# A hybrid layer's input projection: token rows at another stride, one more block scaled late, weight splits ahead of finishing, and finishing in two steps

## The chip, the cores and the metric

The kernel runs on one core of one Trainium2 chip. The metric is the device time of one execution in microseconds, given as the median of several runs; a profiled execution, taken apart from those runs, gives the trace. Five engines work from queues of their own, in order: PE (TensorE, matrix products; its weight loads are listed as PEld), DVE (VectorE), ACT (ScalarE), POOL (GpSimd) and SP (SyncE, which here only issues transfers). Transfers run on 16 DMA engines; loads are issued by SP, stores by POOL.

## The reference

One inference step of one decoder layer for 4096 new tokens and 64 sample tokens (8 sequences of 8), model width 1024, all in fp32:

```
h = rmsnorm(x) * g_pre
z = h @ w_in                      # (4160, 1024) @ (1024, 2816)
out_a = silu(cg) * cb * conv3(cc * ch)            # 256 channels
out_b = silu(ag) * window_attention(q, k, v)      # window 128, 8 heads of 64, 2 kv heads, a sink each
out_c = silu(mg) * memory_attention(mq)           # 4 heads of 64, 256 memory tokens
y = [out_a, out_b, out_c] @ w_out                 # (4160, 1024) @ (1024, 1024)
x = x + rmsnorm(y) * g_post
```

Results are the new x, the keys and values of the last window, the convolution's state, and the memory's keys and values. The result has to be near fp32, so every product of the kernel is made from a number's high part (rounded to the fp32r type) and the rest, three products for one: high by high, high by low, low by high.

## The kernel before

**Two halves.** The first, up to about 1066 us, is the input projection; the second is attention and output projection, ordered by the framework's scheduler. In the first half the order on all engines is written out by hand (a list of numbered steps, each with loads and jobs), and this is where most of the change lies.

**The projection.** The tokens (64 sample tokens first) are five blocks of 832, each two halves of 416. The 22 column tiles of 128 are taken in six groups of up to four (line `GROUPS`): gates (tiles 14 to 17), two convolution groups (0 to 7), memory and attention queries (18 to 21), a one-pair group with keys and values (12, 13), and gates and queries (8 to 11). For each block and group, a step p = 0 to 6 is one of the seven products of Strassen's scheme (in Winograd's form): a sum of weight blocks (A11, S2, A12, S3, S1, A22, S4) by a sum of token blocks (B11, T2, B21, T3, T1, T4, B22). A step has 12 products for each of two column pairs q, on the line that the profile calls L603, 128x416 outputs each; the one-pair group has 12. The first group of the first block is made in eight plain steps instead.

**Weights.** In block 0, and in the first group of block 1, the four raw weight blocks are loaded, POOL and DVE make the sums (`sums`, L166 to L168; `last_sum`, L173), ACT casts to the high part and DVE subtracts (`split_w`, L140 and L141), and POOL stores the split sums (`fill_sum`). Later blocks load the split sums (`load_split`, L153) and split only A11, A12 and A22 (`fill`). Weight buffers go round in a ring of six, two per step.

**Tokens.** During block b-1, the rows of block b are loaded and squared (ACT, L245), POOL makes 1/rms of each (`row_factors`) and stores it (tensor `rowd`), SP loads it back broadcast to all partitions (`row_spread`, L255), and DVE multiplies the transposed tokens by gain and factor (`x_scale`, L199). Then come the sums T1 to T4 and the splits (L218, L219) into `x1`, places of 4 rows of 416 high parts followed by 4 rows of 416 low parts. Block 0 is *unscaled*: ACT applies the gain only (`x_gain`), and DVE multiplies the results by the factors (`z_rows`, L260).

**Ends of steps and groups.** At the end of a step, the accumulators go into z tiles of a ring of three, two for each group: ACT copies at p = 0 and 2 (L612, L616), DVE adds at the others (L610). Finishing a group's z tile is, for gates, tanh (ACT) and a product (DVE), for queries and keys a rounded copy (ACT, L279) and the difference (DVE, L281); POOL stores both. The tile `which=1` is finished at step p = 6 of its group, `which=0` in the step after. For block 0 the sample tokens' columns are also copied to a small buffer `zs`. Within a step, SP gets the step's loads; then come the q = 0 products, half of the jobs (finishing first, then splits and token work), the q = 1 products, the rest of the jobs, and the eviction. So a job that waits holds up everything behind it on its engine, evictions too.

**Block 4** carries the memory's projection and the first chunk of the attention as pieces between its steps (`plan_third`), and near its end the output weights are loaded and split.

The jobs of a step, in `step`, and how the sums of a group that begins at step `s0` are placed, in `plan_weights`:

```
jobs = [*first.pop(i, ()), *jobs_at.pop(i, ())]
half = (len(jobs) + 1) // 2
...
job_at(s0 - 2, *(lambda k=k: split_keep(k) for k in key("A11")))
job_at(s0 - 1, *(lambda b=b, g=g, q=q: sums(b, g, q) for q in qs))
job_at(s0 - 1, *(lambda k=k: fill_sum(k) for k in key("S2")))
```

## Time and profile before

| | |
|---|---|
| median of 3 runs | 1687.2 us (1682.62 to 1687.97) |
| profiled execution | 1681.09 us, span 1679.3 us |
| mean granted clock of PE | 0.967 |
| PE busy | 1552.4 us, 8489 products |
| DVE, ACT, POOL busy | 1012.0, 729.4, 428.8 us |
| input projection | to 1066.5 us |

How rows are read: a row of a group gives line, engine, operation, output and inputs, shape and count, then busy time and mean ns of one, then the idle time just before and what ended it. A row of the timeline is start, length, the same names, and in brackets the idle time before it and what released it. A row of a table by stretch gives the stretch, its length, busy time and count of PE, PEld, DVE, ACT and POOL, the granted clock of PE, the DMA engines' mean busy share, and GB/s.

### The profile page before, as it was taken

The numbers are of one execution on the slowest core, as the hardware profiler recorded it, in microseconds if no ns is written. First come the engines' busy times: TensorE is split into PE (matmuls) and PEld (weight loads), VectorE is DVE, ScalarE is ACT, GpSimd is POOL, SyncE is SP. The second block draws the span as 40 slices with busy tenths as digits, with TensorE's granted clock in tenths as the row PEclk, the third lists the DMA queues.
The fourth block names the chain that finished last, engine by engine and source line by source line (L and its number), as shares of the span: only waits on it lengthen the run. The fifth ranks groups of instructions, "written<-read, shape, count | busy, mean of one in ns | idle before, by whom it ended". The sixth has DMA issues, their size and how long they took to land.

```text
span 1679.3 us, 23937 instructions
## 1 busy us (share of the span) xinstructions
PE 1552.4 (92%) x8489; PEld 1403.4 (84%) x8489; DVE 1012.0 (60%) x1743; ACT 729.4 (43%) x1864; POOL 428.8 (26%) x667
## 2 busy tenths in 40 slices
PE   8799587997999989998998988799999999999998
PEld 8698477997999889997997987678888888888876
DVE  3877587445744466445745544576666666666653
ACT  7434234242433233232432333466565656556542
POOL 1345223001100101001002022363444444444310
PEclk9899798999999999998999999899999999999999
DMA  9468855699677986799787668998767867876332
GB/s 250 162 229 237 279 196 200 220 272 314 230 270 240 276 301 236 233 303 268 252 291 182 197 222 233 288 168 162 159 146 151 166 136 155 167 159 148 126 126 88
DMA packets 167516, 354.30 MB, mean 211 GB/s; under 512 B 21253, under 2 KB 90149, under 8 KB 167365
## 3 DMA queue, kind: packets, MB, share of 16 engines
q1 hardware_dynamic: 116069, 242.06, 48.1%
q0 software_dynamic: 50896, 110.19, 26.8%
q8 instruction: 67, 1.10, 0.3%
q10 hardware_dynamic: 432, 0.53, 0.1%
q14 instruction: 52, 0.43, 0.1%
HBM read 262.93 MB, written 90.77 MB: 211 GB/s over the span
## 4 chain that ended last, share of the span: by engine, by line
PE 44%; issue 2%; DMA 2%; DVE 1%; ACT 1%; POOL 0%; SPq 0%; DVEq 0%; POOLq 0%; ACTq 0%
PE y L1235 21%; PE c L603 8%; PE ws L1003 3%; PE wo L845 2%; PE wt L1026 2%; PE xs L939 2%; PE xt L954 2%; PE wo L975 2%; PE wo L981 1%; DMA vT<-vd 1%; PE mem_acc L517 1%; DMA gpost<-in_gpost 0%; DMA kst<-qd 0%; DMA qd<-zh 0%; DVE z L610 0%
## 5 line engine op out<-in xcount | busy, mean ns | idle before, releaser
L603 PE MATMUL c<-x,w_0S 128*128 128x416 f32 x1392 | 303.9, 370 | 73.3 <-DMA w_0S<-wd_0S 28.6
L1235 PE MATMUL y<-x 128*128 128x512 f32 (+1 forms) x1296 | 369.0, 399 | 0.0
L603 PEld LDWEIGHTS c<-x,w_0S 128*128 128x128 f32 x1392 | 274.4, 200 | 87.2 <-ACT w_0S L140 34.7
L1235 PEld LDWEIGHTS y<-x 128*128 128x128 f32 x1296 | 238.2, 189 | 46.1 <-issue 1.6
L603 PE MATMUL c<-x,w_0A 128*128 128x416 f32 x1140 | 241.4, 362 | 26.7 <-ACT z L612 18.9
L603 PEld LDWEIGHTS c<-x,w_0A 128*128 128x128 f32 x1140 | 219.6, 195 | 35.1 <-ACT z L612 21.4
L610 DVE TENSOR_TENSOR z<-c,z 128x832 f32<-128x832 f32 (+1 forms) x145 | 137.2, 946 | 164.7 <-PE c L603 158.9
L603 PE MATMUL c<-x,w_1S 128*128 128x416 f32 x1152 | 236.4, 354 | 0.0
L603 PEld LDWEIGHTS c<-x,w_1S 128*128 128x128 f32 x1152 | 218.8, 191 | 2.8 <-issue 0.4
L603 PE MATMUL c<-x,w_1A 128*128 128x416 f32 x960 | 196.4, 354 | 0.0
L603 PEld LDWEIGHTS c<-x,w_1A 128*128 128x128 f32 x960 | 180.9, 190 | 2.8 <-issue 1.2
L141 DVE TENSOR_TENSOR w_0A<-wr_0A,w_0A 128x512 fp32r<-128x512 f32 x91 | 64.8, 712 | 121.1 <-ACT w_0A L140 121.1
L1016 ACT ACTIVATE sm<-sm,wnm 128x128 f32<-128x128 f32 x256 | 99.5, 390 | 63.5 <-DVE wnm L1010 63.4
L948 POOL TENSOR_SCALAR xp<-xp,xrd 128x256 f32<-128x256 f32 x128 | 75.9, 601 | 179.2 <-DVE xrd L944 179.1
L1235 PE MATMUL y<-x,parts 128*128 128x512 f32 (+1 forms) x264 | 101.6, 385 | 0.0
L140 ACT CAST w_0A<-wr_0A 128x512 fp32r<-128x512 f32 x91 | 55.9, 616 | 78.9 <-PE c L603 39.1
L940 DVE TENSOR_REDUCE xmx<-xs 128x2 f32<-128x512 f32 x64 | 44.0, 687 | 59.3 <-PE xs L939 59.3
L127 POOL DMA_DIRECT2D md<-th x30 | 16.3, 543 | 246.3 <-DVE th L298 215.9
L1028 ACT COPY wpt<-wt 128x512 f32<-128x512 f32 x64 | 37.1, 583 | 96.0 <-PE wt L1026 95.9
L245 ACT ACTIVATE nat<-nat 104x1024 f32<-104x1024 f32 x40 | 42.3, 1057 | 80.9 <-DMA nat<-in_x_p 78.8
L1003 PEld LDWEIGHTS ws<-kst,q 128*128 128x128 f32 x512 | 70.9, 193 | 7.3 <-DVE z L610 1.5
L1003 PE MATMUL ws<-kst,q 128*128 128x256 f32 x512 | 73.4, 286 | 1.1 <-DVE z L610 1.1
(258 smaller groups left out, 2317.2 us busy)
## 6 DMA issues: line engine op xcount, KB each, us to landing
w_0S<-wd_0S SPq DMA_DIRECT2D x92, 512.0 KB
w_1S<-wd_1S SPq DMA_DIRECT2D x76, 512.0 KB
wr_0A<-in_w_in SPq DMA_DIRECT2D x102, 256.0 KB
q<-qd POOLq DMA_DIRECT2D x64, 384.0 KB, 7.9
wr_1A<-in_w_in SPq DMA_DIRECT2D x85, 256.0 KB
mix<-md SPq DMA_DIRECT2D x16, 1024.0 KB
xr<-in_x_p SPq DMA_DIRECT2D x32, 512.0 KB
nat<-in_x_p SPq DMA_DIRECT2D x39, 416.0 KB
```

Source lines behind the costliest of these rows:

```text
L140: S.copy(w[:, 0], raw)
L141: V.tensor_tensor(w[:, 1], raw, f(w[:, 0]), op=ALU.subtract)
L245: S.activation(t[:RG], t[:RG], AF.Square, accum_out=factors[b][:RG, i : i + 1])
L603: TE.matmul(bank[:, :HW], l, r, start=first and i == 0, stop=last and i == 3 * KH - 1, skip_group_check=more)
L610: add = lambda dst, other: V.tensor_tensor(dst, c, other, op=ALU.add)
L845: TE.matmul(o[cs], v[:, cs], p, start=i == 0, stop=i == n - 1, tile_position=(0, 64 * half))
L940: V.tensor_reduce(mx[:, :nb], s, axis=AX.X, op=ALU.max)
L948: G.tensor_scalar(p[:, i, :], p[:, i, :], rd[:, i : i + 1], 0.5, op0=ALU.mult, op1=ALU.mult)
L1003: TE.matmul(s3[:, hh, :], self.q[:, 4 + 2 * (2 * half + hh) + kvh, i * P : i * P + P], self.kst[:, 2 * kvh + part, i * P : i * P + 2 * P], ...
L1016: S.activation(sm[:, hh, :], sm[:, hh, :], AF.Exp, bias=nm[:, hh : hh + 1], scale=SCALE, accum_out=den[:, hh : hh + 1])
L1028: S.copy(pt, t)
L1235: TE.matmul(acc, self.hl[l][:, k], wo[k][c0 // 512][:, r, c0 % 512 : c0 % 512 + c1 - c0], start=j == 0, stop=j == passes * KT - 1)
```

## The change

1. The split tokens lie in places of their own for high and low parts, each of 4 rows of 448 floats (1792 bytes) of which 416 are used. All moving and all stationary operands of L603 then start at the same address modulo 256.
2. Block 1 is unscaled as well: gains on ACT, `z_rows` on DVE when its groups are finished; its factors are loaded back in its own first group. For blocks 2 to 4 the factors are made at step p = 6 of the second convolution group and loaded back three steps later; the rows are loaded three steps earlier, and the token loads are cut in two and spread over eight steps.
3. Weight splits form a list of their own, first in each step. The sums are made one step earlier, beside A11's split.
4. Finishing takes two steps: rounding or tanh at p = 6 (tile 1) and p = 0 of the next group (tile 0), difference or gate a step later each. The convolution takes four steps.
5. The small copies for sample tokens go; nine loads and two additions late in the attention (`sample_tokens`) take their place.
6. In block 4, the first attention chunk is loaded one step earlier and its pieces begin one step later and follow closer; the second chunk is loaded three steps earlier; output weights' loads and splits are spread otherwise.

```diff
-XS = 2 * KH * HW
+
+XR = 448
+XS = KH * XR
+UNSCALED = 2
...
     def slot(i):
-        return (x6[:, :] if i == 6 else x1[:, i * XS : (i + 1) * XS]).rearrange("p (a k n) -> p a k n", a=2, k=KH)
+        places = [x1[:, n * XS : (n + 1) * XS] for n in range(11)] + [x6[:, n * XS : (n + 1) * XS] for n in range(3)]
+        return [t.rearrange("p (k n) -> p k n", k=KH)[:, :, :HW] for t in places[2 * i : 2 * i + 2]]
...
-    def finish_parts(b, z, idx, zsi):
+    def finish_parts(b, z, idx):
...
-        hi = temp(f"zh{b}_{idx}")[:, :BW].bitcast(F32R)
-        S.copy(hi, z)
-        lo = z.bitcast(F32R)
-        V.tensor_tensor(lo, z, f(hi), op=ALU.subtract)
-        store(f(qd[0, idx, :, tokens(b)]), f(hi))
-        store(f(qd[1, idx, :, tokens(b)]), f(lo))
+        made = []
+
+        def round_():
+            if idx == 0 and b == NBLK - 1:
+                kl = temp("kl")
+                S.copy(kl[:, :P], z[:, BW - P :])
+                store(a["o_kp"], kl[:, :P])
+            hi = temp(f"zh{b}_{idx}")[:, :BW].bitcast(F32R)
+            made.append(hi)
+            S.copy(hi, z)
+            store(f(qd[0, idx, :, tokens(b)]), f(hi))
+
+        def rest():
+            lo = z.bitcast(F32R)
+            V.tensor_tensor(lo, z, f(made[0]), op=ALU.subtract)
+            store(f(qd[1, idx, :, tokens(b)]), f(lo))
+        return round_, rest
+
+    def finish_gate(b, z, idx):
         z = flat(z)
-        th = temp(f"th{b}_{idx}")[:, :BW]
-        S.activation(th, z, AF.Tanh, scale=0.5)
-        V.scalar_tensor_tensor(th, th, 1.0, z, op0=ALU.add, op1=ALU.mult)
-        if b == 0:
-            V.tensor_copy(zs[:, zsi, :], th[:, :NS])
-        store(md[idx, :, tokens(b)], th)
+        made = []
+
+        def tanh():
+            th = temp(f"th{b}_{idx}")[:, :BW]
+            made.append(th)
+            S.activation(th, z, AF.Tanh, scale=0.5)
+
+        def gate():
+            th = made[0]
+            V.scalar_tensor_tensor(th, th, 1.0, z, op0=ALU.add, op1=ALU.mult)
+            store(md[idx, :, tokens(b)], th)
+        return tanh, gate
...
-                    job_at(s0 - 2, *(lambda k=k: split_keep(k) for k in key("A11")))
-                    job_at(s0 - 1, *(lambda b=b, g=g, q=q: sums(b, g, q) for q in qs))
-                    job_at(s0 - 1, *(lambda k=k: fill_sum(k) for k in key("S2")))
-                    job_at(s0, *(lambda k=k: split_keep(k) for k in key("A12")), *(lambda b=b, g=g, q=q: last_sum(b, g, q) for q in qs))
+                    fill_at(s0 - 2, *(lambda k=k: split_keep(k) for k in key("A11")), *(lambda b=b, g=g, q=q: sums(b, g, q) for q in qs))
+                    fill_at(s0 - 1, *(lambda k=k: fill_sum(k) for k in key("S2")))
+                    fill_at(s0, *(lambda k=k: split_keep(k) for k in key("A12")), *(lambda b=b, g=g, q=q: last_sum(b, g, q) for q in qs))
...
-                t = s(2, 0) + i
+                t = s(2, 0) - (3 if b > 1 else 0) + i
                 load_at(t, lambda i=i, b=b: row_load(RJ * b + i))
                 job_at(t + 1, lambda i=i, b=b: row_square(RJ * b + i))
-            job_at(s(3, 2), lambda b=b: row_factors(b))
-            load_at(s(3, 4), lambda b=b: row_spread(b))
+            factors_at, spread_at = (s(2, 6), s(3, 2)) if b >= UNSCALED else (s(3, 2), at[b, 0, 4])
+            job_at(factors_at, lambda b=b: row_factors(b))
+            load_at(spread_at, lambda b=b: row_spread(b))
             for i, o in enumerate(("B11", "B12", "B22", "B21")):
-                load_at(s(3, 1 + i), lambda b=b, o=o: x_load(b, o))
-            for t, o in ((s(3, 6), "B11"), (s(4, 1), "B12"), (s(4, 3), "B22"), (s(4, 5), "B21")):
-                job_at(t, lambda b=b, o=o: x_scale(b, o))
+                for k in range(2):
+                    load_at(s(2, 6) + 2 * i + k + (2 if b == 1 else 0), lambda b=b, o=o, k=k: x_load(b, o, 2 * k, 2 * k + 2))
+            for t, o in ((s(3, 4), "B11"), (s(3, 6), "B12"), (s(4, 2), "B22"), (s(4, 5), "B21")):
+                job_at(t, lambda b=b, o=o: (x_scale if b >= UNSCALED else x_gain)(b, o))
...
-        load_at(n0 + 12, first_chunk)
+        load_at(n0 + 11, first_chunk)
         for n in range(21):
-            third_at(13 + n, lambda: third["chunk"].pop(0)())
-        load_at(n0 + 34, lambda: chunk_load(1))
+            third_at(14 + n * 4 // 5, lambda: third["chunk"].pop(0)())
+        load_at(n0 + 31, lambda: chunk_load(1))
         end = at[NBLK - 1, NG - 1, 0]
-        for p, js in enumerate(((), (0, 1), (2, 3), (4, 5), (6, 7, 8), (9, 10, 11, 12), (13,), (14, 15))):
+        for p, js in ((-1, (0, 1)), (0, (2, 3)), (3, (4, 5, 6, 7)), (4, (8, 9, 10, 11)), (6, (12, 13, 14, 15))):
             for j in js:
-                load_at(end + p - 2, lambda j=j: wo_load(j))
+                load_at(end + p, lambda j=j: wo_load(j))
+        for p, js in enumerate(((), (0, 1), (2, 3), (), (4, 5), (6, 7, 8), (9, 10, 11), (12, 13, 14, 15))):
+            for j in js:
                 job_at(end + p, lambda j=j: wo_split(j))
...
-                n = at[0, 1, 0] if (b, g) == (0, 0) else at[b, g, NP_ - 1] + 1
...
-                scale = lambda which: [lambda b=b, z=z: z_rows(b, z(which))] if b == 0 else []
-                done = lambda which, b=b, g=g, z=z: [lambda: [fn() for fn in finish(b, g, which, z(which))]]
+                scale = lambda which: [lambda b=b, z=z: z_rows(b, z(which))] if b < UNSCALED else []
...
-                    if b == 0:
-                        front_at(n - 1, *scale(1))
-                    front_at(n, *scale(0), make, run(0))
-                    front_at(n + 1, run(1), run(2))
-                elif (b, g) == (0, 0):
-                    front_at(n, *scale(1), *done(1))
-                    front_at(n + 1, *scale(0), *done(0))
+                    front_at(n, *scale(1))
+                    front_at(n + 1, *scale(0), make)
+                    back_at(n + 1, run(0))
+                    front_at(n + 2, run(1))
+                    front_at(n + 3, run(2))
                 else:
-                    front_at(n - 1, *scale(1), *done(1))
-                    front_at(n, *scale(0), *done(0))
+                    for k, which in enumerate((1, 0)):
+                        made = []
+                        make = lambda made=made, b=b, g=g, which=which, z=z: made.extend(finish(b, g, which, z(which)))
+                        run = lambda j, made=made: lambda: [fn() for fn in made[j]]
+                        front_at(n + k, *scale(which), make)
+                        back_at(n + k, run(0))
+                        front_at(n + k + 1, run(1))
...
-        jobs = [*first.pop(i, ()), *jobs_at.pop(i, ())]
+        jobs = [*fills_at.pop(i, ()), *first.pop(i, ()), *back.pop(i, ()), *jobs_at.pop(i, ())]
...
+    def sample_tokens():
+
+        lo = work([P, 4, P], "sm", "zs_lo").rearrange("p a n -> p (a n)")[:, : 7 * NS].rearrange("p (a n) -> p a n", n=NS)
+        cols = lambda x: x[:, :, :NS].rearrange("j p n -> p j n")
...
+        V.tensor_tensor(zs[:, 0:5], zs[:, 0:5], lo[:, 0:5], op=ALU.add)
+        V.tensor_tensor(zs[:, 10:12], zs[:, 10:12], lo[:, 5:7], op=ALU.add)
```

How the order moves, at three places. First POOL where block 1's first group begins (`wr_0` are its raw weights, `w_5` and `z_5` belong to block 0's last group, `wd` are stored sums, `md` and `qd` the results). Before:

```order
L127 DMA md<-th_3_1914 128x832
L127 DMA qd<-zh_2_1920 128x832
L127 DMA qd<-z_5_1_1700 128x832
L166 TENSOR_TENSOR wr_0_0A_1821<-wr_0_0A_1785,wr_0_0A_1821 128x512
L167 TENSOR_TENSOR wr_0_0A_1785<-wr_0_0A_1744,wr_0_0A_1785 128x512
L166 TENSOR_TENSOR wr_0_1A_1823<-wr_0_1A_1787,wr_0_1A_1823 128x512
L167 TENSOR_TENSOR wr_0_1A_1787<-wr_0_1A_1746,wr_0_1A_1787 128x512
L127 DMA wd_0S_1946<-w_0_0S_1943 128x1024
```

and after:

```order
L136 DMA wd_1S_1757<-w_5_1S_1754 128x1024
L136 DMA wd_0S_1830<-w_5_0S_1827 128x1024
L136 DMA wd_1S_1835<-w_5_1S_1832 128x1024
L175 TENSOR_TENSOR wr_0_0A_1810<-wr_0_0A_1774,wr_0_0A_1810 128x512
L176 TENSOR_TENSOR wr_0_0A_1774<-wr_0_0A_1733,wr_0_0A_1774 128x512
L175 TENSOR_TENSOR wr_0_1A_1812<-wr_0_1A_1776,wr_0_1A_1812 128x512
L176 TENSOR_TENSOR wr_0_1A_1776<-wr_0_1A_1735,wr_0_1A_1776 128x512
L136 DMA wd_0S_1911<-w_0_0S_1908 128x1024
L136 DMA wd_1S_1916<-w_0_1S_1913 128x1024
L136 DMA qd<-zh_2_1933 128x832
L136 DMA md<-th_3_1931 128x832
```

The four sums stood behind the stores of the finished tile and now stand ahead of them.

Second, DVE around the fifth group of block 2 (`z_3` is the fourth group's tile, `z_4` the fifth's, `zh` the rounded copy, `x3B` the next block's tokens). Before:

```order
L610 TENSOR_TENSOR z_3_1_4182<-c_3_1_4195,z_3_1_4182 128x2x416
L281 TENSOR_TENSOR z_3_1_4182<-z_3_1_4182,zh_4_4378 128x832
L281 TENSOR_TENSOR z_3_1_4182<-z_3_1_4182,zh_6_4383 128x832
L199 SCALAR_TENSOR_TENSOR x3B_4192<-x3B_4192,gpre,rb_4303 128x416 x4
L610 TENSOR_TENSOR z_3_0_4226<-c_3_4_4308,z_3_0_4226 128x2x416
L281 TENSOR_TENSOR z_3_0_4226<-z_3_0_4226,zh_3_4418 128x832
L281 TENSOR_TENSOR z_3_0_4226<-z_3_0_4226,zh_5_4423 128x832
L141 TENSOR_TENSOR w_4_0A_4428<-wr_4_0A_4334,w_4_0A_4428 128x512
L199 SCALAR_TENSOR_TENSOR x3B_4232<-x3B_4232,gpre,rb_4303 128x416 x4
L610 TENSOR_TENSOR z_4_0_4454<-c_4_1_4437,z_4_1_4431 128x416
```

and after:

```order
L639 TENSOR_TENSOR z_3_1_4191<-c_3_1_4204,z_3_1_4191 128x2x416
L209 SCALAR_TENSOR_TENSOR x3B_4201<-x3B_4201,gpre,rb_4243 128x416 x4
L639 TENSOR_TENSOR z_3_0_4237<-c_3_4_4318,z_3_0_4237 128x2x416
L150 TENSOR_TENSOR w_4_0A_4433<-wr_4_0A_4348,w_4_0A_4433 128x512
L296 TENSOR_TENSOR z_3_1_4191<-z_3_1_4191,zh_4_4397 128x832
L296 TENSOR_TENSOR z_3_1_4191<-z_3_1_4191,zh_6_4400 128x832
L296 TENSOR_TENSOR z_3_0_4237<-z_3_0_4237,zh_3_4440 128x832
L296 TENSOR_TENSOR z_3_0_4237<-z_3_0_4237,zh_5_4443 128x832
L639 TENSOR_TENSOR z_4_0_4469<-c_4_1_4452,z_4_1_4446 128x416
```

The two differences on `z_3_1` stood ahead of the last eviction into `z_3_0`; they now follow it and the split of `w_4_0A`, with the other two behind them, and the eviction into `z_4_0`, which takes over `z_3_1`'s buffer, comes straight after.

Third, SP in the fourth group of block 2 (`rb` is the load of the factors, `w_3_0S` a load of split sums, `x3B` a load of tokens, `wr_4` raw weights). Before:

```order
L189 DMA x3B_4265<-in_xt 128x4x96
L189 DMA x3B_4265<-in_xt 128x4x320
L153 DMA w_3_0S_4299<-wd_0S_1370 128x1024
L153 DMA w_3_1S_4301<-wd_1S_1387 128x1024
L255 DMA rb_4303<-rowd_80 128x832
L189 DMA x3B_4305<-in_xt 128x4x128
L189 DMA x3B_4305<-in_xt 128x4x288
L148 DMA wr_4_0A_4334<-in_w_in 128x512
L153 DMA w_4_0S_4364<-wd_0S_1463 128x1024
```

and after:

```order
L162 DMA w_3_0S_4193<-wd_0S_1216 128x1024
L162 DMA w_3_1S_4195<-wd_1S_1221 128x1024
L157 DMA wr_3_0A_4197<-in_w_in 128x512
L157 DMA wr_3_1A_4199<-in_w_in 128x512
L199 DMA x3B_4201<-in_xt 128x2x96
L199 DMA x3B_4201<-in_xt 128x2x320
L162 DMA w_3_0S_4239<-wd_0S_1267 128x1024
L162 DMA w_3_1S_4241<-wd_1S_1272 128x1024
L265 DMA rb_4243<-rowd_73 128x832
L199 DMA x3B_4201<-in_xt 128x2x96
L199 DMA x3B_4201<-in_xt 128x2x320
L157 DMA wr_4_0A_4276<-in_w_in 128x512
```

The load of the factors stood right behind the fourth group's S4 sums and ahead of a whole token load; it now stands two steps earlier, between the halves of the second token load, and the S4 sums come behind it.

176 lines of the change are left out of this document (97 added, 79 removed).

## The prediction

> **What bounds the kernel now.** The page's first part and the busy time by stretch come first. The stretches are cut at the starts of products; the first column is the stretch, then its length, and busy time with (count) per engine.
>
> ```profile
> PE 1552.4 (92%) x8489; PEld 1403.4 (84%) x8489; DVE 1012.0 (60%) x1743; ACT 729.4 (43%) x1864; POOL 428.8 (26%) x667
> 8.22:48.11 39.89, 38.41 (x193) 37.16 (x193) 20.34 (x20) 30.42 (x50) 8.55 (x6) 0.96 0.84 227
> 48.11:96.68 48.57, 36.10 (x169) 33.87 (x168) 39.58 (x40) 19.58 (x25) 15.66 (x18) 0.89 0.55 194
> 170.82:210.66 39.84, 20.08 (x85) 18.06 (x84) 23.63 (x36) 7.74 (x15) 8.97 (x14) 0.74 0.81 286
> 210.66:253.12 42.46, 35.38 (x170) 33.87 (x169) 34.25 (x35) 16.74 (x24) 11.33 (x15) 0.92 0.53 191
> 253.12:299.27 46.15, 36.77 (x169) 34.68 (x168) 32.52 (x36) 20.01 (x28) 13.56 (x20) 0.89 0.57 204
> 362.68:423.30 60.62, 50.77 (x254) 47.98 (x254) 33.32 (x47) 15.95 (x27) 7.77 (x12) 0.97 1.00 299
> 423.30:550.11 126.81, 126.81 (x674) 125.83 (x672) 69.89 (x72) 46.55 (x62) 7.53 (x14) 1.00 0.76 250
> 550.11:607.86 57.75, 49.90 (x254) 48.40 (x253) 33.22 (x47) 15.60 (x26) 7.76 (x12) 0.97 1.03 299
> 734.67:794.20 59.53, 52.55 (x254) 50.86 (x253) 33.40 (x47) 15.90 (x26) 7.75 (x12) 0.91 1.00 298
> 1066.50:1679.30 612.80, 599.90 (x3665) 484.46 (x3665) 394.80 (x989) 340.67 (x1243) 250.59 (x408) 0.99 0.71 153
> ```
>
> TensorE is the bound wherever it is not made to wait. From 423.30 to 550.11 it runs without a gap: 672 products in 126.81 us, 188.7 ns each. A group of seven steps with 24 products each therefore costs 31.7 us at least, the one-pair group 15.9. Against that, 8.22 to 299.27 (block 0 and the first group of block 1: 192 + 5 x 168 + 84 = 1116 products, 210.6 us) takes 291.05 us, so 80 us are lost there. The three stretches of 58 to 61 us are the fourth and fifth groups of blocks 1 to 3, 252 products or 47.6 us each: 35 us lost. The last stretch, attention and the output projection, is 98% busy; the change leaves its instructions on PE in the same order but for the first pieces, and I give it nothing. The profiled execution took 1681.1 us (span 1679.3), the median of the runs is 6.1 above it; I sum against 1681.1 and add 6 at the end.
>
> **Addresses.** The change gives every token row the stride 1792 in place of 1664, and both operands of each L603 product the same address modulo 256. Rows of one step in the undisturbed stretch, and of seven back-to-back products of 512 columns late in the kernel:
>
> ```profile
> 434.62 2.43 PE L603 MATMUL c<-x,w_1A 128*128 128x416 f32 x12
> 436.88 2.43 PE L603 MATMUL c<-x,w_0S 128*128 128x416 f32 x12
> ...
> 1311.21 1.75 PE L1235 MATMUL y<-x 128*128 128x512 f32 x7
> 1312.80 1.12 PE L1003 MATMUL ws<-kst,q 128*128 128x256 f32 x8
> ```
>
> Twelve products take 436.88 - 434.62 = 2.26 us, 188.5 ns each. Seven products of 512 columns take 1.59 us, 227 ns each, or 184.5 ns for 416 columns. So the most that equal addresses can give is 4 ns on each of 4644 products, 19 us; the least is nothing, or a loss of a few us if the new stride is worse. Half of the products have equal addresses already (1664 is six and a half times 256, so every other row matches), and no row shows two speeds. I take a third of the range, -6 us.
>
> The Trainium skill's page "TensorE: Matmul & The Clock Gate" (Part 2, "Step-by-step: what each phase is for") speaks against this part: it says that TensorE reads the moving operand and the next weights through two independent ports, so that loading weights takes no read bandwidth from the running product. By that rule the term would be 0 and the sum 6 us higher; the 4 ns between the rows above do not decide it, since they compare products of different length.
>
> **Block 0 and the first group of block 1.** Here the weights' sums and splits are made for the first time, on POOL, DVE and ACT, and PE waits for them:
>
> ```profile
> 77.00 3.96 PE L603 MATMUL c<-x,w_0S 128*128 128x416 f32 x12 [8.43 <-DVE z L610]
> 187.79 4.56 PE L603 MATMUL c<-x,w_0S 128*128 128x416 f32 x12 [14.55 <-ACT w_0S L140]
> 261.55 1.06 PE L603 MATMUL c<-x,w_0S 128*128 128x416 f32 x2 [3.75 <-ACT w_0S L140]
> ...
> 254.64 0.55 POOL L127 DMA_DIRECT2D md<-th  x1 [11.86 <-DVE zs L300]
> 256.36 1.30 POOL L166 TENSOR_TENSOR wr_0A<-wr_0A,wr_0A 128x512 f32<-128x512 f32 x1
> 260.30 1.60 POOL L167 TENSOR_TENSOR wr_1A<-wr_1A,wr_1A 128x512 f32<-128x512 f32 x1
> ...
> 259.03 1.73 DVE L168 TENSOR_TENSOR wr_0A<-wr_0A,wr_0A 128x512 f32<-128x512 f32 x1 [3.53 <-POOL wr_0A L167]
> ```
>
> The chain is visible at 254 to 262. POOL holds the previous group's stores until DVE has finished that group (11.86 us idle), only then makes the four sums (256.36 to 261.9), DVE waits for them, ACT's split waits for DVE, and PE for ACT. The change puts the sums a step earlier and each step's splits ahead of the finishing, so the chain starts about a step (4.5 us) earlier and no longer behind the stores. The stall goes; what is late next is DVE's own work, which does not shrink: 39.58 us in the second stretch, 34.25 and 32.52 in the fifth and sixth groups' rows, 23.63 in the one-pair group. With every other wait gone, each stretch would end at the larger of its DVE time and PE's floor: 48.57 to 39.6, 39.84 to 23.6, 42.46 to 34.3, 46.15 to 32.5, a gain of 47. These four rows hold 66 of the 80 us lost; of the other 14 perhaps 10 can go as well, so 57 at most, and nothing at the least. A boundary keeps part of its wait, since finishing in the step after needs the last eviction first. I take 9 + 9 + 6 + 8 in the four and 3 in the rest, -35.
>
> Block 1 unscaled: x_scale's 16 instructions on DVE go to ACT, and z_rows comes to block 1.
>
> ```profile
> L199 DVE SCALAR_TENSOR_TENSOR x1B<-x1B,gpre,rb 128x416 f32<-128x416 f32 x16 | 9.3, 646 | 0.0
> L260 DVE TENSOR_TENSOR z<-z,rb 128x1664 f32<-128x1664 f32 x10 | 19.8, 1983 | 0.3
> L298 DVE SCALAR_TENSOR_TENSOR th<-th,z 128x832 f32<-128x832 f32 x30 | 30.1, 1024 | 19.9 <-ACT th L297 19.8
> L612 ACT COPY z<-c 128x832 f32<-128x832 f32 x24 | 20.4, 849 | 16.1 <-PE c L603 16.0
> L141 DVE TENSOR_TENSOR w_0A<-wr_0A,w_0A 128x512 fp32r<-128x512 f32 x91 | 64.8, 712 | 121.1 <-ACT w_0A L140 121.1
> ```
>
> DVE loses 9.3 us in block 0, where it is the bound (in the -35), and gains ten z_rows and two half ones, 22 us, in block 1, where it is busy for little over half of the time. At a group's boundary this lies on a chain: last eviction 1.0, two splits 1.4, two gates 2.0, z_rows 2.0, two tanh on ACT 1.8, then ACT's eviction 0.85. That is 9.1 us after the new group's first step began, and PE wants the bank again at its third step, 9.05 us in. So each of block 1's six boundaries may cost 0 to 2 us: I take +5 for all.
>
> **Blocks 1 to 3, fourth and fifth groups.** SP issues the loads in order, and one of them waits for the row factors' store:
>
> ```profile
> SPq L255 <- DMA rowd<-r: 48.5, 5, 10.6
> DMA to landing us min/median/max: 9.1/13.6/15.4
> ...
> 580.42 2.52 PE L603 MATMUL c<-x,w_0S 128*128 128x416 f32 x12 [2.98 <-DMA w_0S<-wd_0S]
> 592.21 4.06 PE L603 MATMUL c<-x,w_0S 128*128 128x416 f32 x12 [4.72 <-DMA w_0S<-wd_0S]
> ```
>
> The first row is SP's waits for the factors (total, times, longest); the second, from the factors' tensor, is how long their store takes; then two rows of PE in block 2. PE waits 7.7 of the 10.2 us lost here in block 2 for S weights: the longer wait is for a load that stands behind the factors' on SP, the shorter for one ahead of it, late with the DMA full (share 1.03). After the longer one twelve products take 4.06 us in place of 2.43. The change computes the factors three steps (13.6 us) ahead of the load and not two (none of it in block 1), so SP waits 0 to 2 us; the row loads go into the stretch before, with a DMA share of 0.76, and the token loads are spread, which helps the shorter. That removes about 9 us per block. But a new wait comes. Finishing in two steps stores the fourth group's low parts a step later, and the fifth group's second eviction writes the same buffer:
>
> ```profile
> 586.16 1.02 DVE L610 TENSOR_TENSOR z<-c,z 128x832 f32<-128x832 f32 x1
> ...
> 585.06 2.43 PE L603 MATMUL c<-x,w_0A 128*128 128x416 f32 x12
> ...
> 581.84 0.54 POOL L127 DMA_DIRECT2D qd<-z  x1
> DMA to landing us min/median/max: 6.2/7.5/9.5
> ```
>
> Before, the second store issues at 581.84 and lands by about 589, and the eviction that needs it comes at 596. After, the two differences follow the last eviction and a split: 587.2 + 0.7 + 2.0 = 589.9, landing at 597.9 with the median 7.5 (here 6.2 to 9.5). PE needs the evicted bank at the group's fourth step, 585.06 + 6.8 = 591.9. A stall of 4 to 6 us in each block takes the place of the 9 that go: three blocks, -14 in all (0 to -24). DVE waits there too, with the next token scaling and a split queued behind it; the rows give it slack (33 of 58 us). Block 4 has the same new stall; I count +2 for it beside waits that it has there already.
>
> **Block 4.**
>
> ```profile
> 925.98 0.69 PE L903 MATMUL vtp<-ident,vT 128*128 128x128 f32 x2 [9.44 <-DMA vT<-vd]
> ...
> 1037.45 16.94 SPq L587 DMA_DIRECT2D wor<-in_w_out  x7
> 1044.80 4.53 PE L603 MATMUL c<-x,w_0S 128*128 128x416 f32 x12 [4.72 <-DMA w_0S<-wd_0S]
> 1059.05 3.83 PE L603 MATMUL c<-x,w_0S 128*128 128x416 f32 x12 [2.78 <-DVE x L594]
> ```
>
> The value load goes a step earlier and the piece that needs it a step later, 9 us together against a wait of 9.44: -9. The output weights' loads, seven of which hold SP for 16.94 us ahead of an S load, are spread, and their splits moved apart: of 7.5 us in the last two waits and the slow products behind them I take -6 (0 to -10). New are nine small loads and two additions late in the attention; DVE waits for them once, 0 to 5 us, in a place where PE has two quarters of a block of other work: +0.
>
> **Sum.** -6 - 35 + 5 - 14 + 2 - 9 - 6 = -63: 1681.1 - 63 = 1618, and 1624 as the median of runs.
>
> **Rivals.** (a) Block 0 stays as it is, because DVE's in-order work sets it and moving splits ahead only moves the wait to the finishing and its evictions: for it, DVE's 39.58 of 48.57 us in the second stretch; against it, 23.63 of 39.84 in the one-pair group. Without the -35: 1659. Chance 0.20. (b) The equal addresses give nothing, because a weight load does not disturb the running product (the mechanism that the steady 188.5 ns would also show): 1630, chance 0.15 as the only miss. The Trainium skill's "TensorE: Matmul & The Clock Gate" is the page with this rule. (c) The change doesn't do what it says in the fourth and fifth groups: the DMA share there is 1.00 to 1.03, and S loads stay late though SP is free, with the new stall beside: 1638 without the -14, and 1655 with the new stall on top in four blocks. Chance 0.10. (d) The other side: the new buffer wait in the fifth group takes long. The landing of these stores over the whole run:
>
> ```profile
> DMA to landing us min/median/max: 2.7/6.8/24.4
> ```
>
> If a store in the fourth group lands after 21 us rather than 7.5, all five blocks lose 13.5 more, 68 us, and the gain is gone; at 24.4 us it would be 1624 + 5 x 17 = 1709. For it speaks the full DMA, against it 9.5 as the longest landing in the stretch above. Chance 0.11. (e) Better than forecast, block 0 down to DVE's time: 1603 or less, chance 0.09. The forecast itself, 1608 to 1640, has 0.35.
>
> **Range and chances.** The range runs from 1590 (block 0 at its bound, equal addresses worth more than 6) to 1672 (nothing in block 0 and a part of the new stalls uncovered). Within 0.3%, 5 us, no run of this kernel can tell a difference. Below 1682 lie (a), (b), (c), (e) and the forecast with a sliver of (d): faster 0.86; 0.03 for 1682 to 1692; slower 0.11.
>
> **What would show it.** In the changed profile the steps in undisturbed stretches should last 4.50 us rather than 4.53; SP's wait for the factors' store should fall from 48.5 us to below 15; the 9.44 wait for the values should be gone; POOL's sums should stand ahead of the stores in block 0; and a new wait of PE for the eviction of the fifth group, 4 to 6 us, should appear in every block. It is wrong if block 0's first 299 us stay above 285, or if that new wait exceeds 15 us.

## The result, and the profile after

The changed kernel takes 1681.79 us (median; 1676.45 to 1701.13), the kernel before, run beside it, 1683.71 us (1675.15 to 1689.69). The ratio is 0.9997, with a 95% interval of 0.9976 to 1.0018: no difference. The forecast was 1624.

The profiled execution took 1680.55 us, its span 1678.5. PE is busy for 1547.6 us, 5 us less than before, and the time that it saves in some stretches it loses in others. Cut at the starts of the same products (block 4 at the end of its last one), before and after:

| stretch, us | before | after | forecast for it |
|---|---|---|---|
| start | 8.2 | 6.8 | |
| block 0 and first group of block 1 | 291.1 | 286.9 | -35 |
| rest of blocks 1 to 3 | 529.7 | 541.1 | -14 and +5 |
| block 4 | 236.3 | 226.8 | +2 - 9 - 6 |
| attention and output projection | 614.1 | 616.8 | 0 |

The forecast's -6 for the addresses is spread over the three middle rows.

Blocks 1 to 3 lost 11.5 us, and not where a loss had been expected. The table by stretch of the kernel after (stretch, length, busy time and count of PE, PEld, DVE, ACT and POOL, granted clock, DMA share, GB/s) has first the counterparts of the prediction's rows: second stretch, one-pair group, its sixth group, first group of block 1, then the fourth and fifth groups of blocks 1, 2 and 3. The last two rows have no counterpart there: the first group of block 2 (31.7 us before) and the second of block 4 (40.1 before).

```profile
47.86:102.86 55.00, 37.13 (x169) 35.26 (x169) 38.94 (x38) 21.16 (x28) 13.64 (x17) 0.81 0.53 171
179.15:205.47 26.32, 17.98 (x86) 17.42 (x85) 13.60 (x18) 14.62 (x25) 5.98 (x11) 0.81 1.00 347
205.47:246.22 40.75, 35.33 (x169) 33.56 (x168) 32.88 (x34) 16.24 (x22) 18.66 (x19) 0.92 0.58 218
246.22:293.73 47.51, 33.48 (x169) 32.52 (x169) 34.35 (x35) 19.48 (x25) 7.61 (x14) 0.86 0.56 207
360.35:417.60 57.25, 51.36 (x253) 49.65 (x253) 38.30 (x50) 13.16 (x21) 7.79 (x12) 0.94 0.90 284
554.88:608.59 53.71, 49.57 (x254) 48.45 (x253) 32.84 (x47) 12.23 (x18) 4.89 (x9) 0.97 0.87 297
745.01:800.26 55.25, 49.44 (x253) 48.18 (x253) 32.80 (x47) 12.42 (x18) 6.63 (x11) 0.97 0.88 290
449.24:490.27 41.03, 33.44 (x170) 32.77 (x169) 21.56 (x20) 15.35 (x18) 3.25 (x6) 0.92 0.59 203
870.79:919.64 48.85, 41.59 (x206) 39.03 (x204) 19.52 (x30) 14.00 (x27) 6.27 (x12) 0.93 0.60 198
```

Block 0 became uneven: the one-pair group fell from 39.84 to 26.32, the second stretch rose from 48.57 to 55.00. The fourth and fifth groups gained 3.4, 4.0 and 4.3 us, nearly as forecast. But the first group of a block, 31.7 us before in blocks 2 and 3, now takes 41.0 and 40.2. Nearly all of that is one wait of PE in each, 7.6 and 5.9 us for an eviction on ACT, and the slow products behind it. PE's waits over the whole run before, then after (what PE waited for; total, times, longest):

```profile
PE c L603 <- DMA w_0S<-wd_0S: 28.6, 8, 5.0
PE c L603 <- ACT w_0S L140: 24.2, 4, 14.6
PE c L603 <- ACT z L612: 18.9, 7, 5.0
PE c L603 <- DVE z L610: 18.8, 9, 8.4
PE vtp L903 <- DMA vT<-vd: 9.4, 1, 9.4
```

```profile
PE c L632 <- ACT z L641: 51.7, 14, 13.1
PE c L632 <- DVE z L639: 25.9, 9, 11.9
PE mem_acc L544 <- ACT wh L532: 7.3, 1, 7.3
PE c L632 <- DMA w_0S<-wd_0S: 7.2, 6, 2.0
PE ws L1044 <- DMA q<-qd: 6.5, 1, 6.5
```

The waits that the change was to remove are gone or much smaller: loads of S weights from 28.6 to 7.2, their split from 24.2 to 2.7, the values' 9.4 altogether. In their place PE waits 51.7 us, not 18.9, for evictions on ACT: 27.9 instead of 13.4 up to 290 us, and 23.8 instead of 5.5 behind. The timeline of block 3's first group in the kernel after shows what holds one; PE's rows first, then ACT's, then POOL's:

```profile
644.75 2.42 PE L632 MATMUL c<-x,w_0S 128*128 128x416 f32 x12
647.01 2.42 PE L632 MATMUL c<-x,w_1S 128*128 128x416 f32 x12
655.32 4.53 PE L632 MATMUL c<-x,w_0A 128*128 128x416 f32 x12 [5.89 <-ACT z L641]
...
643.26 0.90 ACT L316 ACTIVATE th<-z 128x832 f32<-128x832 f32 x1 [1.90 <-issue]
652.15 0.88 ACT L291 CAST zh<-z 128x832 fp32r<-128x832 f32 x1 [7.99 <-DMA md<-th]
652.94 1.57 ACT L228 CAST x<-x3T 128x1664 fp32r<-128x1664 f32 x1
654.42 0.84 ACT L641 COPY z<-c 128x832 f32<-128x832 f32 x1
...
645.61 0.54 POOL L136 DMA_DIRECT2D md<-th  x1 [5.94 <-DVE th L320]
```

Finished tiles pass through a ring of three temporaries (`temp`, pool `t`). This group finishes four: gate, query, gate, query. The fourth, the rounded copy at 652.15, takes the temporary of the first gate, and so needs that gate's store landed. In two steps the gate is made a step after its tanh, its store leaves POOL at 645.61, and ACT stands still for 7.99 us until it has landed. The copy of p = 0 is queued behind it on ACT, and PE stands at p = 2 without a free bank. The same place before:

```profile
643.36 0.87 ACT L279 CAST zh<-z 128x832 fp32r<-128x832 f32 x1
...
638.70 0.54 POOL L127 DMA_DIRECT2D md<-th  x1 [27.19 <-DVE th L298]
```

The store had left at 638.70, 4.66 us ahead of the copy at 643.36, and had landed after 2.7 us, so 2.0 us were to spare. (Stores into `md` took 2.7 to 13.5 us to land in this run, 4.3 in the median.) In the changed kernel the store leaves 6.9 us later and takes 6.5 us to land.

### The profile page after: what moved, and what is told of

Read it like the earlier page. It is cut to its first block, busy times and chain, and to the rows that moved or that the text cites. A ratio compares the mean times of both kernels' runs of the same rounds, so it can differ in the third digit from the quotient of the medians.

```text
span 1678.5 us, 23984 instructions
## 1 busy us (share of the span) xinstructions
PE 1547.6 (92%) x8489; PEld 1401.6 (83%) x8489; DVE 1022.3 (61%) x1737; ACT 740.1 (44%) x1872; POOL 423.4 (25%) x664
## 5 line engine op out<-in xcount | busy, mean ns | idle before, releaser
L632 PE MATMUL c<-x,w_0S 128*128 128x416 f32 x1392 | 295.2, 363 | 41.1 <-DVE z L639 22.8
L632 PEld LDWEIGHTS c<-x,w_0S 128*128 128x128 f32 x1392 | 269.4, 196 | 51.3 <-issue 20.8
L632 PE MATMUL c<-x,w_0A 128*128 128x416 f32 x1140 | 245.0, 366 | 58.4 <-ACT z L641 51.7
L989 POOL TENSOR_SCALAR xp<-xp,xrd 128x256 f32<-128x256 f32 x128 | 79.3, 628 | 192.5 <-DVE xrd L985 192.5
L316 ACT ACTIVATE th<-z 128x832 f32<-128x832 f32 x30 | 26.4, 895 | 100.3 <-DVE z L270 41.2
```

What stands on the lines that cost most here:

```text
L632: TE.matmul(bank[:, :HW], l, r, start=first and i == 0, stop=last and i == 3 * KH - 1, skip_group_check=more)
L989: G.tensor_scalar(p[:, i, :], p[:, i, :], rd[:, i : i + 1], 0.5, op0=ALU.mult, op1=ALU.mult)
```

## Experiments

Spans and stretches below are of profiled executions; ratios are to the kernel before, run beside each.

### Is the two-step finishing what costs? (e1, e2, e11)

The theory: the change gains some 40 us, and finishing in two steps takes them back through the three temporaries. The rival: nothing was gained, because equal addresses and the earlier splits give nothing and the waits only changed their names.

e1 frees the temporary earlier and leaves the two steps: the gate's product goes to `z`, whence it is stored, so the temporary is free once DVE has read it.

```diff
-            V.scalar_tensor_tensor(th, th, 1.0, z, op0=ALU.add, op1=ALU.mult)
-            store(md[idx, :, tokens(b)], th)
+            V.scalar_tensor_tensor(z, th, 1.0, z, op0=ALU.add, op1=ALU.mult)
+            store(md[idx, :, tokens(b)], z)
```

> The changed kernel, but the gate's product is written into the z tile and stored from there, so that the buffer of the tanh is free when DVE has read it and not when its store has landed. Theory A (the three temporary buffers: with finishing in two steps the store of a gate comes a step later, the group's fourth rounding or tanh waits for it to land, and ACT's eviction and PE wait behind): ACT's 24 us of waits for the stores of th go, the second steps of the first groups, 17.8, 12.3 and 10.6 us in blocks 1 to 3, fall to 5 to 6, and the time to 1640 to 1655. Theory B (block 0 is bound by DVE's work, and the two-step finishing costs nothing): 1675 to 1685, as the changed kernel.

e2 finishes gates, queries, keys and values in one step, at the step of their first half; all else is as after.

```diff
-                        front_at(n + k, *scale(which), make)
-                        back_at(n + k, run(0))
-                        front_at(n + k + 1, run(1))
+                        front_at(n + k, *scale(which), make, run(0), run(1))
```

> The changed kernel with gates, queries, keys and values finished in one step again (the convolution stays in three). Theory A: both the waits for th's stores and the wait for the fourth group's low parts go, so the gains of the other parts come out: 1630 to 1650. Theory B: block 0 stays at 285 us or more, the rest gains 10 to 20: 1660 to 1675. Theory C (splits first delay evictions on their own): 1675 or more.

e11 is the other way round: the kernel before, with its gates, queries, keys and values finished in two steps, and nothing else of the change.

```diff
...
-                    front_at(n - 1, *scale(1), *done(1))
-                    front_at(n, *scale(0), *done(0))
+                    for k, which in enumerate((1, 0)):
+                        t = n + k - (0 if (b, g) == (0, 0) else 1)
...
+                        front_at(t, *scale(which), make)
+                        back_at(t, run(0))
+                        front_at(t + 1, run(1))
```

> The kernel before with only the finishing of gates, queries, keys and values put into two steps (convolution as it was). Theory A: ACT waits for the stores of th at the first and second groups' starts as in the changed kernel, and PE for the fourth group's low parts: 25 to 45 us slower, 1705 to 1725. Theory B: within 5 us of before.

| us | before | after | e1 | e2 | e11 |
|---|---|---|---|---|---|
| median | 1683.71 | 1681.79 | 1655.08 | 1636.99 | 1713.12 |
| ratio | | 0.9997 | 0.9875 | 0.9767 | 1.0216 |
| 95% interval | | 0.9976 to 1.0018 | 0.9819 to 0.9932 | 0.9721 to 0.9812 | 1.0174 to 1.0257 |
| block 0, first group of block 1 | 291.1 | 286.9 | 284.1 | 284.5 | 299.7 |
| rest of blocks 1 to 3 | 529.7 | 541.1 | 529.2 | 514.6 | 555.7 |
| first group of block 3 | 31.7 | 40.2 | 33.5 | 31.6 | 39.0 |
| block 4 | 236.3 | 226.8 | 220.0 | 215.1 | 240.1 |

The theory holds from both sides. Undoing the two steps takes 43.2 us off the profiled span (1678.5 to 1635.3); adding them to the kernel before costs 34 (1713.12 against 1679.09 of the runs beside it). And e11 shows the same wait at the same place, block 3's first group, ACT's row and PE's:

```profile
672.38 0.88 ACT L283 CAST zh<-z 128x832 fp32r<-128x832 f32 x1 [5.50 <-DMA md<-th]
...
676.58 3.83 PE L620 MATMUL c<-x,w_0A 128*128 128x416 f32 x10 [4.39 <-ACT z L629]
```

ACT's waits for `md<-th` are gone in e1 and e2 but for 0.4 us; the kernel before has 0.2. In the kernel after they are, in the view of ACT's waits:

```profile
ACT th L316 <- DMA md<-th: 23.9, 5, 6.8
ACT zh L291 <- DMA md<-th: 17.5, 4, 8.0
```

Of the 43 us e1 gives back 25.5 by the spans (1678.5 to 1653.0), so the gates' temporaries are the larger part. What makes up the other 17.7 was not taken apart. In e1 the gates leave from the `z` tiles too, and the evictions on ACT and DVE that wait for stores out of these tiles stand for 39.9 us, against 22.3 in the kernel after and 17.4 in e2, so a part is e1's own. In the one-step kernel the first group of block 3 stands at 31.6, in e1 at 33.5, where the wait is for a `z` tile whose low part is still being stored:

```profile
646.76 0.85 ACT L645 COPY z<-c 128x832 f32<-128x832 f32 x1 [2.99 <-DMA qd<-z]
```

Hence the rest of the change does gain, about 44 us of span (1679.3 to 1635.3): 6.6 in block 0, 15.1 in blocks 1 to 3, 21.1 in block 4. The rival falls. What the two steps cost lies almost all behind block 0 (2.4 us of the 43 are in it): of PE's waits for evictions on ACT e2 keeps 27.1 us of the 27.9 up to 290 us, and 9.2 of the 23.8 behind.

### Equal addresses (e3)

Rows dense at 1664 bytes again, all else as after:

```diff
-        return [t.rearrange("p (k n) -> p k n", k=KH)[:, :, :HW] for t in places[2 * i : 2 * i + 2]]
+        return [t[:, : KH * HW].rearrange("p (k n) -> p k n", k=KH) for t in places[2 * i : 2 * i + 2]]
```

> The changed kernel with token rows 1664 bytes apart again, in the same places, so that half of the L603/L632 products have unequal addresses modulo 256. If equal addresses matter (-6 us in the prediction's sum): undisturbed steps 4.53 us instead of 4.52, time 2 to 8 us more than the changed kernel. If they don't: within 2 us of it, steps alike.

Measured 1684.23 us, ratio 1.0026 (0.9998 to 1.0055), against 0.9997 (0.9976 to 1.0018): 5 us, which the intervals do not tell from nothing. The undisturbed steps show a small difference. In e3 first, then in the kernel after:

```profile
512.75 2.43 PE L632 MATMUL c<-x,w_1S 128*128 128x416 f32 x12
515.02 2.43 PE L632 MATMUL c<-x,w_0A 128*128 128x416 f32 x12
517.28 2.43 PE L632 MATMUL c<-x,w_1A 128*128 128x416 f32 x12
```

```profile
449.24 2.42 PE L632 MATMUL c<-x,w_0A 128*128 128x416 f32 x12
451.50 2.42 PE L632 MATMUL c<-x,w_1A 128*128 128x416 f32 x12
453.76 2.42 PE L632 MATMUL c<-x,w_0S 128*128 128x416 f32 x12
```

Twenty-four products take 4.53 us in e3 and 4.52 with equal addresses. Over undisturbed groups of 168 it is 31.73 us against 31.64, in some groups 31.36: 188.9 ns a product against 188.3 or 186.7. Over the 4644 products of the projection that is 2.5 us, or 10 if all ran at the lower value. The starts of single products show more than the rows, each of which merges 12. In e3's undisturbed groups a product on the first or third of the moving operand's four rows takes 187.2 ns on average from its start to the next, one on the second or fourth, which start 128 bytes off the others modulo 256, 190.6; in the kernel before it is 187.4 and 190.0. In the kernel after, with rows of 1792 bytes, the two kinds take nearly the same, 188.2 and 187.8, though not 187.2. So the rows' place counts; whether it is the match with the weights' address or the row's own start, no run shows. The Trainium skill's page "TensorE: Matmul & The Clock Gate" (Part 2, "Step-by-step: what each phase is for") says that weight loads take no read bandwidth from the running product; against it the runs have at most these few ns, and that they come from weight loads is not shown. Why some groups reach 31.36 is open.

### Splits first, sums earlier, block 1 unscaled (e4 to e7)

e4 (on the kernel after) and e6 (on e2) put the weights' splits behind the finishing again:

```diff
-        jobs = [*fills_at.pop(i, ()), *first.pop(i, ()), *back.pop(i, ()), *jobs_at.pop(i, ())]
+        jobs = [*first.pop(i, ()), *back.pop(i, ()), *fills_at.pop(i, ()), *jobs_at.pop(i, ())]
```

> The changed kernel with the weight splits behind the finishing again in each step's jobs (the sums still a step earlier). Theory A: stores of gates issue 1 to 2 us earlier, so the waits in blocks 1 to 4 shrink a little, and block 0 loses part of what splits first gave: 1675 to 1695. Theory C (splits first are what delays evictions): 1650 to 1665.

> The one-step version with splits behind the finishing (sums a step earlier). If splits first hold up evictions (DVE and ACT wait for the sums with everything behind them): groups 2 and 4 of block 0 fall from 49.8 and 44.2 to 48 and 39, time 1625 to 1635. If splits first are what takes 13 us out of the one-pair group: that group goes back to 38 and the time to 1640 to 1650.

e5 is e2 with the sums back one step:

```diff
-                    fill_at(s0 - 2, *(lambda k=k: split_keep(k) for k in key("A11")), *(lambda b=b, g=g, q=q: sums(b, g, q) for q in qs))
-                    fill_at(s0 - 1, *(lambda k=k: fill_sum(k) for k in key("S2")))
+                    fill_at(s0 - 2, *(lambda k=k: split_keep(k) for k in key("A11")))
+                    fill_at(s0 - 1, *(lambda b=b, g=g, q=q: sums(b, g, q) for q in qs), *(lambda k=k: fill_sum(k) for k in key("S2")))
```

> The one-step version with the weight sums of block 0 back where they stood (one step before the group; splits still first). Theory D (the sums wait for the last raw weight block, which is loaded only a step before them, so a step earlier in the order gains nothing): block 0 and the first group of block 1 within 5 us of the 284.5 of the one-step version, time 1632 to 1645. Theory E (the sums' place is what gave the gain in block 0's one-pair group, 39.9 to 26.7 us): that group back above 35, time 1645 to 1657.

e7 is e2 with only block 0 unscaled (`UNSCALED = 1`); block 1's rows and tokens are then loaded as early as the other blocks'.

> The one-step version with only block 0 unscaled; rows, factors and token loads of block 1 are timed like those of blocks 2 to 4. If z_rows in block 1 costs at the boundaries (prediction: +5): the first group of block 2 falls from 36.4 to 32, but block 0 gets 9 us of DVE work back: 1632 to 1645. If DVE's work in block 0 is the bound: 1645 to 1655, with block 0's last two groups and block 1's first each some 3 us longer.

| | e4 | e6 | e5 | e7 | e2 |
|---|---|---|---|---|---|
| ratio | 0.9998 | 0.9783 | 0.9751 | 0.9786 | 0.9767 |
| 95% interval | 0.9966 to 1.003 | 0.9745 to 0.9821 | 0.9716 to 0.9787 | 0.9742 to 0.983 | 0.9721 to 0.9812 |
| block 0, first group of block 1, us | 292.4 | 283.8 | 278.0 | 291.9 | 284.5 |

No interval tells e4 from the kernel after, nor e5, e6 or e7 from e2. These were the parts that were to give 35 us in block 0, and by these runs each is worth a few us at most: the order of splits and finishing little, the earlier sums nothing (a profile of the later ones is even 6.5 us shorter in block 0). Splits first mostly move the loss: in e4 the one-pair group is back at 37.8 us (26.3 in the kernel after), while the second stretch falls from 55.0 to 51.5 and the fourth group from 42.7 to 39.5. Why the earlier sums do not help is in e2's timeline of POOL:

```profile
134.46 1.42 POOL L175 TENSOR_TENSOR wr_0A<-wr_0A,wr_0A 128x512 f32<-128x512 f32 x1 [6.58 <-DMA wr_0A<-in_w_in]
```

The sums wait for the last raw block to land; in e5, a step later in the order, they still wait 5.16 us for it. The unscaled block 1 shows in two places of e7's profile: block 0 is 7.4 us longer with block 1's tokens scaled, and the first group of block 2 takes 31.6 us, against 36.4 in e2, where block 1's factors stand on the path of its last tiles.

### Block 4 and the token loads (e8, e12)

e8 is e2 with block 4's loads and pieces timed as before (the output weights' included), e12 is e2 with the rows and factors of blocks 2 to 4 and the token loads and scalings of blocks 1 to 4 timed as before.

```diff
-        load_at(n0 + 11, first_chunk)
+        load_at(n0 + 12, first_chunk)
...
-            third_at(14 + n * 4 // 5, lambda: third["chunk"].pop(0)())
-        load_at(n0 + 31, lambda: chunk_load(1))
+            third_at(13 + n, lambda: third["chunk"].pop(0)())
+        load_at(n0 + 34, lambda: chunk_load(1))
...
```

> The one-step version with block 4's loads, pieces and output weights timed as before the change. By the prediction's sum (-9 for the values, -6 for the output weights): 1650 to 1654, and block 4 longer by 15 of the 21 us that it gained. If block 4's gain came from elsewhere (splits first, equal addresses): 1635 to 1642.

```diff
-                t = s(2, 0) - (3 if b > 1 else 0) + i
+                t = s(2, 0) + i
...
-            factors_at, spread_at = (s(2, 6), s(3, 2)) if b >= UNSCALED else (s(3, 2), at[b, 0, 4])
+            factors_at, spread_at = (s(3, 2), s(3, 4)) if b >= UNSCALED else (s(3, 2), at[b, 0, 4])
...
```

> The one-step version with rows, factors and token loads of blocks 2 to 4 timed as before the change. By the prediction (the SP wait for the factors and the full DMA cost 9 us in each of blocks 1 to 3): blocks 1 to 3 10 to 18 us longer, 1647 to 1655. If the gain there came from splits first: 1635 to 1641.

e8: ratio 0.9864 (0.9835 to 0.9894), block 4 at 234.4 us, 19.3 above e2. e12: 0.9914 (0.9882 to 0.9945), rest of blocks 1 to 3 at 533.6, 19.0 above e2. Both cost somewhat more than expected (15, and 10 to 18), and both times, some 1660 and 1662 us, lie above the ranges named. So these two parts carry most of the gain, and by the mechanisms of the prediction: in e8 the values' wait is back with 7.0 us, and PE's waits for S weights in block 4 rise from 2.0 to 8.7. The waits of SP and PE in e12, then in e2:

```profile
SPq L265 <- DMA rowd<-r: 37.6, 4, 10.7
...
PE c L631 <- DMA w_0S<-wd_0S: 24.4, 10, 6.4
```

```profile
SPq L265 <- DMA rowd<-r: 11.1, 1, 11.1
...
PE c L632 <- DMA w_0S<-wd_0S: 3.6, 4, 1.4
```

### What holds block 0 (e9, e10, e13, e14)

Even in e5, 278.0 us stand against 210.6 of products. PE's and ACT's waits in e5 from 5 to 290 us:

```profile
PE c L632 <- ACT z L641: 28.4, 5, 10.4
...
ACT th L316 <- DVE z L270: 27.3, 6, 6.9
```

The theory: in an unscaled block the tanh of the group's second tile waits for its factors (`z_rows`, L270), these stand on DVE behind the splits, and ACT's copy of p = 0 stands behind the tanh. The rival: DVE has too much work. e9 is e5 with the second tile of blocks 0 and 1 finished one step later (the convolution's tanh too); the work is the same.

```diff
-                    back_at(n + 1, run(0))
+                    if b < UNSCALED:
+                        front_at(n + 2, run(0))
+                    else:
+                        back_at(n + 1, run(0))
...
-                        front_at(n + k, *scale(which), make, run(0), run(1))
+                        front_at(n + k, *scale(which), make)
+                        front_at(n + k + (1 if b < UNSCALED and which == 0 else 0), run(0), run(1))
```

> The version of e5 (one step, sums where they stood) with the second tile of a group in the two unscaled blocks finished a step later, behind ACT's first eviction of the next group; the multiplication by the factors stays where it is. Theory F (in unscaled blocks ACT's eviction stands behind a tanh that waits for z_rows, which stands behind splits and sums on DVE; PE waits 28 us for it in block 0): that wait falls below 10 us and the time to 1612 to 1625. Theory G (DVE's work as such bounds block 0; the wait only moves): 1630 to 1642.

e10 is e5 with `z_rows` cut to one token, e13 is e9 without POOL's two sums, e14 is both. These three leave work out, so their results are other numbers; they only price it.

> The version of e5 with z_rows cut to one token: the results of blocks 0 and 1 are left without their row factors; 22 instructions of 1 to 2 us on DVE are left out. Theory F and theory G both expect 1605 to 1622 and no wait of ACT for z_rows; block 0 with the first group of block 1 then at 255 to 265 us from 278. If it stays above 272, neither is right and the sums' chain from the raw loads sets block 0.

> The version of e9 without POOL's two sums for each weight pair (the raw blocks stand in for S1 and S3, so results are other numbers; 22 instructions of 1.3 to 2.8 us on POOL are left out, all of DVE's and ACT's work stays). Theory H (the sums' chain, POOL then DVE then ACT, and DVE's slower work beside POOL's set what is left in block 0): block 0 with the first group of block 1 falls from 273 us to 250 to 260. Theory I (the eviction and finishing chain on DVE and ACT sets it): 266 to 274.

> As e13, and without the row factors of blocks 0 and 1 on all but one token (z_rows cut to one column). If both chains matter: block 0 at 235 to 250 us, near PE's floor of 211 plus the start; if neither does: above 262, and the rest is the plain chain of splits that every group of block 0 has.

| us | e5 | e9 | e10 | e13 | e14 |
|---|---|---|---|---|---|
| median | 1638.16 | 1626.43 | 1617.21 | 1611.7 | 1601.61 |
| ratio | 0.9751 | 0.971 | 0.9637 | 0.9595 | 0.9535 |
| 95% interval | 0.9716 to 0.9787 | 0.9664 to 0.9755 | 0.9591 to 0.9683 | 0.9495 to 0.9694 | 0.946 to 0.9609 |
| block 0, first group of block 1 | 278.0 | 273.3 | 268.9 | 261.2 | 250.8 |

e13 and e14 were executed twice each. e9, at 1626.43 us the fastest of those that leave nothing out, is 3% faster than both kernels, though its interval overlaps e5's. Its waits of PE from 5 to 290 us show the theory half right:

```profile
PE c L632 <- DVE z L639: 22.2, 6, 6.7
PE c L632 <- ACT z L641: 7.0, 3, 4.2
```

The wait for ACT's evictions falls from 28.4 to 7.0 us, that for DVE's rises from 8.6 to 22.2: the late factors now stand in front of DVE's own evictions. Leaving out work helps more: the factors 9.1 us in block 0 (e5 to e10), POOL's sums 12.2 (e9 to e13). In e10 and e13 block 0 came out between the ranges named beforehand, so neither the factors nor the sums set it alone. The sums cost DVE time too. A split beside POOL's sums in e10, DVE and then POOL, and in e14, without the sums:

```profile
45.36 1.90 DVE L150 TENSOR_TENSOR w_0A<-wr_0A,w_0A 128x512 fp32r<-128x512 f32 x1
...
45.41 1.29 POOL L175 TENSOR_TENSOR wr_0A<-wr_0A,wr_0A 128x512 f32<-128x512 f32 x1
```

```profile
43.71 0.69 DVE L150 TENSOR_TENSOR w_0A<-wr_0A,w_0A 128x512 fp32r<-128x512 f32 x1 [0.18 <-ACT w_0A L149]
```

With both left out block 0 still takes 40 us more than its products. What makes these was not taken apart.

## Why the prediction was wrong

The sum said -63, the profiled time moved by -0.5. Three things make up the difference: +43 for the two-step finishing, which the sum held only as a wait in the fifth group; +28 for block 0, sized at -35 and worth -6.6; and some 9 us by which the other parts gave more.

**The step that failed: "But a new wait comes".** The prediction asked what a later store would hold up and found the `z` tile of the fifth group, 4 to 6 us a block. That wait came, a little smaller: DVE waits 12.0 us in three places, up to 4.7, for `qd<-z`, and PE at the same step of the fifth group, 0.29 us in block 1 and more in blocks 2 and 3,

```profile
597.87 6.36 PE L632 MATMUL c<-x,w_0S 128*128 128x416 f32 x24 [3.05 <-DVE z L639]
...
789.61 6.34 PE L632 MATMUL c<-x,w_0S 128*128 128x416 f32 x24 [3.42 <-DVE z L639]
```

The later store is not its only cause, though. In e11 the two steps alone make ACT and DVE wait 19.3 and 6.0 us for `qd<-z`, where the evictions of the kernel before have no such wait. But in e2, where these stores leave in one step, the same rows of blocks 2 and 3 still wait 2.21 and 2.88 us. In e12, where the waits for S weights are back, DVE waits 0.2 us in all for `qd<-z`; so PE probably meets this wait as soon as nothing else makes it late.

The larger cost is another: later stores leave from the temporaries too, and those were not followed, though a ring of three with four tiles a group reuses one in every group of gates and queries. Both rows that price it stood in the trace of before: store at 638.70, reuse at 643.36, with 2.0 us to spare. Making the gate a step later moves the store by 6.9 us (645.61 for 638.70; 0.7 of it is the later start of that group), past the point of reuse, in a place where PE has one step until it lacks a bank. The landing also grew, from 2.7 to 6.5 us here and from 4.3 to 6.4 in the median of the stores into `md`; why was not taken apart. Rival (d) had the right sign and the wrong buffer, and so the wrong price. Its 24.4 us is not a store's, either: the view of `qd` counts the attention's loads from it too, and the 70 stores of that run landed within 9.7 us.

**Block 0, -35.** Worth -4.1 in the kernel after and -6.6 without the two steps. The reading of the chain was right (POOL's sums behind the stores, then the split: 24.2 us of waits became 2.7), and the one-pair group gained 13.5 where 9 was taken. But the 9, 6 and 8 of the other three did not come: +6.4, -1.7 and +1.4. The step that failed is "What is late next is DVE's own work": bounded by busy time (39.6 of 48.6 us), it took each stretch to end at the larger of that and PE's floor, and left out that evictions and factors stand in that queue behind the splits. DVE's busy time in the whole stretch fell from 203.9 to 192.7 us, and the waits went to evictions instead: PE's waits for those of ACT from 5 to 290 us rose from 13.4 to 27.9. Rival (a) said so, with a chance of 0.20.

**"Wrong if block 0's first 299 us stay above 285."** They did: 286.9 with the first group of block 1. The other condition, a new wait above 15 us in the fifth group, did not come about.

**Addresses, -6.** 0.5 to 2 ns of 188.9 ns a product: 2.5 to 10 us, and e3's 5 us lies in it. The steps take 4.52 us rather than the forecast 4.50. The reading "no row shows two speeds" was wrong, since a row merges 12 products: the single ones had two, 187.4 and 190.0 ns. All products at the faster of these would have given 6 us, so the size taken was a plausible one by luck, and not reached.

**Block 1's boundaries, +5.** Without the two steps block 2's first group, where block 1's last tiles are finished, takes 36.4 us for 31.7: +4.7, all in one boundary of the six.

**Blocks 1 to 3, fourth and fifth groups, -14.** Measured -11.7 in the kernel after, -18.3 in e2; e12 gives 19.0 us back. That the first number is near the forecast is partly luck: the sum charged the two steps some 4 us a block here for a wait that mostly stays without them, and left out what else they cost. SP's wait for the factors' store fell from 48.5 to 12.1, below the 15 named. Rival (c) falls.

**Block 4, +2 - 9 - 6 = -13.** Measured -9.4, and -21.1 without the two steps. The +2 is the mis-sized term, for the reason above: in the second group four gates in a row need the three temporaries, and the memory's pieces stand behind them on ACT. ACT's row and PE's:

```profile
880.87 0.90 ACT L316 ACTIVATE th<-z 128x832 f32<-128x832 f32 x1 [6.21 <-DMA md<-th]
...
882.73 1.22 PE L544 MATMUL mem_acc<-wh,mparts 128*128 128x512 f32 x2 [7.26 <-ACT wh L532]
```

The values' 9.44 went, but in the kernel after the queries' load came late in its place:

```profile
943.61 2.04 PE L1044 MATMUL ws<-kst,q 128*128 128x256 f32 x8 [6.45 <-DMA q<-qd]
```

The output weights gave more than the 6: the last group of block 4 fell from 47.1 to 35.6, of which 1.9 come back right behind it, where PE's first product of the attention waits 3.0 us for the last eviction and not 1.1.

## What to carry to other kernels

When a change makes a store later, list every buffer that the store reads, find for each the next writer in the trace, and compare the gap between issue and reuse with the landing time: here 4.66 us lay between issue and reuse, the landings ran from 2.7 to 13.5 us, and the store was moved by 6.9. An instruction that waits for a buffer on an in-order queue costs what stands behind it, so look for the evictions in that queue first. And busy time of an engine bounds what a reordering can gain only if the order in its queue is also good: 80 us of idle PE against a DVE that was 70% busy gave 7.

## What the runs showed of the hardware

- A DVE operation on two operands in the core's memory took 1.90 us while POOL worked on two of its own, and 0.69 us alone; which adds 1.2 us on the engine that block 0 waits for. The Trainium skill's page "SBUF — State Buffer" ("Who interferes with whom") says that such a pair contends for a shared port; the rows agree.
- Products of 416 columns took 190.6 ns on every other row of the moving operand, whose start lies 128 bytes off the others modulo 256 (rows 1664 bytes apart), and 187.2 on the rest, in the undisturbed groups of e3. With rows 1792 bytes apart the two kinds are nearly alike, and the mean is 188.3 ns, in some groups 186.7; why there are two values is open.
